# Four small transfers of a triangular inverse, issued from GpSimd's queue in place of SyncE's, in a one-core decoder layer

## The chip, the cores and the metric

The kernel runs on one core of one Trainium2 chip. The metric is the time of one execution on the device in microseconds; lower is better. The kernel before ran three times: 2893.89, 2886.44 and 2890.0 us, median 2890.0 us.

## What is computed

One layer of a hybrid decoder, for a prompt of 512 tokens and a sample group of 8 sequences with 4 tokens each (544 columns together), all in float32 with D = 2048. Cut to the part that the change touches, the gated DeltaNet heads:

```python
decay = jnp.exp(jnp.where(incl, cum[..., :, None] - cum[..., None, :], -jnp.inf))
kk = jnp.einsum('nbhid,nbhjd->nbhij', kc, kc)
lower = jnp.where(strict, bc[..., :, None] * kk * decay, 0.0)
rhs = jnp.concatenate([vc * bc[..., None], kc * (bc * jnp.exp(cum))[..., None]], axis=-1)
sol = lax.linalg.triangular_solve(lower + jnp.eye(c, dtype=f32), rhs, left_side=True, lower=True, unit_diagonal=True)
...
def step(state, inp):
    u_i, w_i, qk_i, q_i, k_i, g_i = inp
    v_new = u_i - jnp.einsum('bhcd,bhde->bhce', w_i, state)
    o_i = jnp.einsum('bhcd,bhde->bhce', q_i, state) + jnp.einsum('bhij,bhje->bhie', qk_i, v_new)
    state = g_i * state + jnp.einsum('bhcd,bhce->bhde', k_i, v_new)
    return state, o_i
```

Around it stand one combined projection, stick-breaking attention with 8 heads, the output projection, a cross attention over 256 memory tokens and a SwiGLU block.

## The kernel before

Activations lie transposed, 128 features on the partitions and 544 tokens along the free dimension. A product with a float32 weight is made of three float32r products (high times high, high times low, low times high). `weights` loads 512 KB of a weight at a time from SyncE's queue (L201), ScalarE casts the high part (`wh`, L206), VectorE subtracts it for the low part (`wl`, L207), and `products` issues the matmuls (L218). There are three raw buffers and four of each part, so that the load of a piece waits for VectorE to be done with an older one.

The dense projections set the pace. Everything else of a head is a generator (`sb_head`, `gdn_head`, `gdn_sample`, `sb_sample`) that the class `Side` steps forward between matmuls: each `yield cost, lat` names the TensorE time that the step took and a latency in microseconds before which its next step isn't taken. With it the program text puts the side work among the projections; the instructions then stand in one fixed order on each engine, and an engine that comes to an instruction whose input is missing waits there, with everything behind it.

`gdn_head` runs for 8 heads (called head 0 to head 7 here), between about 490 and 1000 us of the span. For each it makes the 128 x 128 matrices of four chunks (`gt`, L1087 and L1088) and calls `invert`, which calls `invert16` for the 16 x 16 blocks on the diagonal. `invert16` needs the 32 blocks (4 chunks with 8 blocks each) with one block on each partition. It gets them by way of DRAM:

- L890: GpSimd copies identities into `t`, half of the tile `g16`.
- L892: `gt` (128 partitions, 4 x 128 values each) is written to the scratch array `scr[0]`, 256 KB.
- L894: the 32 diagonal blocks are read back to `g`, 32 partitions with 16 rows of 16 values, 32 KB.
- L896: GpSimd changes the sign.
- L899 and L900: VectorE solves the blocks row by row, 15 multiplications and 15 reductions, interleaved with its other work.
- L903: the solved blocks are written to the diagonal of `scr[1]` or `scr[2]` (zero elsewhere), 32 KB.
- L906: the whole array is read back to the tile `T`, 256 KB, followed by `yield 0.0, 8`.
- L924: TensorE transposes `T`; ScalarE copies it to `TT` (L926), and the levels 16, 32 and 64 are built from it by matmuls (L960 and L965).

Each of L894, L903 and L906 waits for what stands before it: the transfer before, or VectorE. All four go out on SyncE's queue, which also issues the weights (L201), the cache pages (L787) and the states of the sample group. GpSimd's queue holds in this stretch the product of the gate `cv` (L870, the end of a SiLU), small clears (L1020, the three columns ahead of a convolution, read by L1035), copies of the convolution's tail (L1026), `qd` (L1074), the decay products (L1087, L1092), clears of the windows for the sample values (L740) and the convolution of the sample group (L1168, L1170). The only transfers on GpSimd's queue are those of L2126 in the SwiGLU stage, after 2383 us.

Of the kernel before, what the change touches and what calls it, by code (L numbers as in the profile page):

```python
# [51 lines left out]
def bc(ap, shape):  # L52
    return ap.broadcast_to(shape)
# [819 lines left out]
def invert16(c, gt):  # L873

    nc = c.nc
    gt16 = c.tt("g16")
    g, t, prod = gt16[:32, 0:256], gt16[:32, 256:512], c.tt("p16")[:32]
    src, dst = c.scr[0], c.scr[1 + c.inv % 2]  # L880
    c.inv += 1

    def whole(x):
        return x.rearrange("(a x) -> a x", a=4)[:, : P * P].rearrange("a (j i) -> j a i", i=P)

    def blocks(x):
        return x.rearrange("(n x) -> n x", n=32)[:, : 16 * P].rearrange("n (r i) -> n r i", i=P)[:, :, :16]

    gv, tv = (x.rearrange("p (r i) -> p r i", r=16) for x in (g, t))
    nc.gpsimd.tensor_copy(t, c.id16)  # L890
    yield 0.0, 1.0
    nc.sync.dma_start(whole(src), v3(gt))  # L892
    yield 0.0, 2.5
    nc.sync.dma_start(gv, blocks(src))  # L894
    yield 0.0, 2.5
    nc.gpsimd.tensor_scalar(g, g, -1.0, None, ALU.mult)  # L896
    for i in range(1, 16):
        p3 = prod[:, : i * i].rearrange("p (n j) -> p n j", n=i)
        nc.vector.tensor_mul(p3, tv[:, :i, :i].rearrange("p j n -> p n j"), bc(gv[:, :i, i : i + 1].rearrange("p j o -> p o j"), [32, i, i]))  # L899
        nc.vector.tensor_reduce(tv[:, i, :i], p3, mybir.AxisListType.X, ALU.add)  # L900
        if i % 4 == 3:
            yield 0.0, 1.2 + i / 8
    nc.sync.dma_start(blocks(dst), tv)  # L903
    yield 0.0, 2.5
    tr = c.tt("T")
    nc.sync.dma_start(v3(tr), whole(dst))  # L906
    yield 0.0, 8
    return tr


def invert(c, gt, nc_, levels, res):
# [17 lines left out]
    if levels[0] == 16:  # L929
        tr = yield from invert16(c, gt)  # L930
        tt = transposed(tr)
    else:
        ps = transposes(c, gt, nc_)
        tr, tt = c.tt("T"), c.tt("TT")
        nc.vector.tensor_mul(v3(tr, nc_), v3(ps, nc_), wide(c.m1))
        nc.vector.tensor_sub(v3(tr, nc_), wide(c.ident), v3(tr, nc_))
        nc.gpsimd.tensor_mul(v3(tt, nc_), gv, wide(c.m1t))
        nc.gpsimd.tensor_sub(v3(tt, nc_), wide(c.ident), v3(tt, nc_))
# [54 lines left out]
def v3(t, n=4):  # L993
    return t[:, : n * P].rearrange("p (a d) -> p a d", a=n)
# [1441 lines left out]
```

## Time and profile before

| what | value |
|---|---|
| three runs | 2893.89, 2886.44, 2890.0 us; median 2890.0 |
| profiled execution, its own time | 2890.46 us |
| its span, first to last instruction | 2888.8 us |
| mean granted clock of TensorE | 0.996 of full speed |
| TensorE matmul busy | 2825.7 us, 98% of the span |
| weight load busy (beside the matmuls) | 2717.5 us, 94% |
| VectorE busy | 2013.4 us, 70% |
| ScalarE busy | 1447.1 us, 50% |
| GpSimd busy | 728.0 us, 25% |
| hardware queue of SyncE (q1) | 600600 packets, 384.64 MB |
| software queue (q0) | 22176 packets, 42.90 MB |

The table is read from the top: the span is nearly filled by TensorE, and the rest of the engines stand beside it. A wait counts where it ends a wait of TensorE. Times in the sections below count from the start of the span; the letter q behind an engine's name (SPq, POOLq) marks its instruction queue, and PEld is TensorE's weight load, which goes ahead of each matmul.

### The profile page before, as it was taken

To read this page: it belongs to the slowest core of one execution; us is meant where nothing else is said; L and a number is where in the kernel's file an instruction comes from. 1 tells how busy PE (TensorE), PEld (TensorE's weight loads), DVE (VectorE), ACT (ScalarE), POOL (GpSimd) and SP (SyncE) were. 2 spreads that over 40 slices of the span, in tenths; PEclk is the share of its full clock that TensorE was granted. 3 is DMA by queue.
4 is the path that set the end of the run, shared out by engine and by line. 5 is a ranking of instruction groups with operands and counts; after the bars stand their busy time and mean duration, and the time that the engine had idled before them with its cause. 6 is when DMAs were issued, how large, how long until landed. Compare 5 with 4: busy or idle time off the path is not lost. (4 is left out here: it accounts for less than half of the span.)

```text
span 2888.8 us, 57077 instructions
## 1 busy us (share of the span) xinstructions
PE 2825.7 (98%) x22442; PEld 2717.5 (94%) x22442; DVE 2013.4 (70%) x3168; ACT 1447.1 (50%) x2760; POOL 728.0 (25%) x858
## 2 busy tenths in 40 slices
PE   8999999999999999999989999999999999999998
PEld 7998888888989999999789999999999999999998
DVE  5554435577777654446588888888888887888886
ACT  5445435454444354434654444444444446555675
POOL 3122212123213110003333333433433334121200
PEclk9999999999999999999999999999999999999999
DMA  7334453544342464533535455545545559876653
GB/s 227 98 90 136 132 155 116 157 118 141 109 135 87 138 202 149 152 101 104 189 121 161 146 154 174 168 148 165 164 146 157 157 152 274 246 223 182 198 166 91
DMA packets 632693, 442.72 MB, mean 153 GB/s; under 512 B 36107, under 2 KB 559704, under 8 KB 632424
## 3 DMA queue, kind: packets, MB, share of 16 engines
q1 hardware_dynamic: 600600, 384.64, 44.8%
q0 software_dynamic: 22176, 42.90, 4.8%
q10 hardware_dynamic: 9648, 11.54, 1.1%
q8 instruction: 176, 2.88, 0.4%
q14 instruction: 93, 0.76, 0.1%
HBM read 359.23 MB, written 79.75 MB: 152 GB/s over the span
## 5 line engine op out<-in xcount | busy, mean ns | idle before, releaser
L2061 PE MATMUL gu<-pr,wh 128*128 128x272 f32 x4944 | 675.1, 289 | 6.7 <-ACT pr L1690 3.0
L2061 PEld LDWEIGHTS gu<-pr,wh 128*128 128x128 f32 x4944 | 643.4, 189 | 8.4 <-ACT pr L1690 3.4
L218 PE MATMUL mm<-ah,wh 128*128 128x272 f32 (+1 forms) x2464 | 542.2, 300 | 6.5 <-ACT ah L334 4.2
L218 PE MATMUL mm<-al,wh 128*128 128x272 f32 (+1 forms) x2464 | 519.6, 290 | 0.7 <-DVE al L249 0.7
L218 PE MATMUL mm<-ah,wl 128*128 128x272 f32 (+1 forms) x2464 | 513.8, 289 | 0.1
L1941 PE MATMUL bank<-pr,wh 128*128 128x272 f32 x2464 | 466.5, 289 | 0.9 <-ACT bank L1969 0.9
L207 DVE TENSOR_TENSOR wl<-wr,wh 128x512 fp32r<-128x512 f32 (+1 forms) x340 | 244.1, 721 | 239.8 <-ACT wh L206 228.6
L218 PEld LDWEIGHTS mm<-ah,wh 128*128 128x128 f32 (+1 forms) x2464 | 386.6, 188 | 25.8 <-issue 12.1
L218 PEld LDWEIGHTS mm<-al,wh 128*128 128x128 f32 (+1 forms) x2464 | 388.1, 188 | 3.0 <-DVE al L249 0.9
L1941 PEld LDWEIGHTS bank<-pr,wh 128*128 128x128 f32 x2464 | 386.3, 188 | 2.9 <-ACT bank L1969 2.7
L218 PEld LDWEIGHTS mm<-ah,wl 128*128 128x128 f32 (+1 forms) x2464 | 385.2, 188 | 3.2 <-issue 1.7
L2061 PE MATMUL gu<-pr,wl 128*128 128x272 f32 x2472 | 362.9, 289 | 1.9 <-issue 1.8
L206 ACT CAST wh<-wr 128x512 fp32r<-128x512 f32 (+1 forms) x340 | 207.7, 614 | 307.9 <-PE mm L218 255.4
L1941 PE MATMUL bank<-pr,wl 128*128 128x272 f32 x1232 | 354.8, 288 | 0.0
L2061 PEld LDWEIGHTS gu<-pr,wl 128*128 128x128 f32 x2472 | 330.6, 189 | 2.3 <-issue 2.0
L1839 DVE TENSOR_TENSOR wl<-sum,wh 128x1024 fp32r<-128x1024 f32 x172 | 220.3, 1281 | 76.9 <-ACT wh L1835 76.9
L1941 PEld LDWEIGHTS bank<-pr,wl 128*128 128x128 f32 x1232 | 232.0, 188 | 0.0
L1835 ACT CAST wh<-sum 128x1024 fp32r<-128x1024 f32 x172 | 180.4, 1049 | 78.3 <-PE gu L2061 47.2
L1839 DVE TENSOR_TENSOR wl<-raw,wh 128x1024 fp32r<-128x1024 f32 x133 | 202.2, 1521 | 15.4 <-ACT wh L1835 13.5
L1835 ACT CAST wh<-raw 128x1024 fp32r<-128x1024 f32 x133 | 139.9, 1052 | 102.4 <-PE gu L2061 93.1
L2126 POOL DMA_DIRECT2D pr<-hT x154 | 81.8, 546 | 254.1 <-PE bank L1941 229.2
L1828 DVE TENSOR_TENSOR sum<-raw,sum 128x1024 f32<-128x1024 f32 x86 | 135.8, 1579 | 0.9
(530 smaller groups left out, 4152.5 us busy)
## 6 DMA issues: line engine op xcount, KB each, us to landing
raw<-in_w_gate_up SPq DMA_DIRECT2D x176, 512.0 KB
wr<-in_w_in SPq DMA_DIRECT2D x108, 512.0 KB
raw<-in_w_down SPq DMA_DIRECT2D x176, 256.0 KB
hT<-hs SPq DMA_DIRECT2D x154, 272.0 KB
pr<-hT POOLq DMA_DIRECT2D x154, 272.0 KB, 6.5
page<-in_cache_sb_k SPq DMA_DIRECT2D x128, 128.0 KB
page<-in_cache_sb_v SPq DMA_DIRECT2D x64, 256.0 KB
wr<-in_w_out SPq DMA_DIRECT2D x32, 512.0 KB
```

The costliest lines, as they stand in the source:

```text
L206: nc.scalar.copy(hi[:, :m, :n], raw[:, k : k + m, :n])
L207: nc.vector.tensor_sub(lo[:, :m, :n], raw[:, k : k + m, :n], hi[:, :m, :n].bitcast(F32))
L218: c.nc.tensor.matmul(ps[:n, h, :HT], l[:, :n], r[:, h * HT : (h + 1) * HT], start=first and i == 0, stop=last and i == 2,)
L1828: self.f.c.nc.vector.tensor_sub(self.a[q], self.a[x], self.a[y])
L1835: self.f.c.nc.scalar.copy(self.hi[q], self.left(q))
L1839: self.f.c.nc.vector.tensor_sub(self.lo[q], self.left(q), self.hi[q].bitcast(F32))
L1941: self.c.nc.tensor.matmul(self.c.bank[bank][:, o], t[x][:, s, i * P : (i + 1) * P], pairs[i].op[q][r], start=new and not (i or n), stop=se ...
L2061: self.c.nc.tensor.matmul(bank, w[:, i * P : (i + 1) * P], self.pairs[i].op[q][r], start=start and n == 0, stop=n == 23, skip_group_check= ...
L2126: self.c.nc.gpsimd.dma_start(t, self.hT[2 * g + pair, :, max(0, 2 * n - 1) + k])
```

## The change

The four calls in `invert16` are issued by `nc.gpsimd` in place of `nc.sync`. Shapes, scratch arrays, waits and the steps of the generator stay as they are.

```diff
     nc.gpsimd.tensor_copy(t, c.id16)
     yield 0.0, 1.0
-    nc.sync.dma_start(whole(src), v3(gt))
+    nc.gpsimd.dma_start(whole(src), v3(gt))
     yield 0.0, 2.5
-    nc.sync.dma_start(gv, blocks(src))
+    nc.gpsimd.dma_start(gv, blocks(src))
     yield 0.0, 2.5
     nc.gpsimd.tensor_scalar(g, g, -1.0, None, ALU.mult)
 ...
-    nc.sync.dma_start(blocks(dst), tv)
+    nc.gpsimd.dma_start(blocks(dst), tv)
     yield 0.0, 2.5
     tr = c.tt("T")
-    nc.sync.dma_start(v3(tr), whole(dst))
+    nc.gpsimd.dma_start(v3(tr), whole(dst))
     yield 0.0, 8
     return tr
```

The 32 transfers leave SyncE's queue and stand in GpSimd's. On SyncE, at the end of head 5's inversion, the piece of the difference is (`scr` is the scratch array, `wr` a raw weight, `cumrow` the decay row of the next head, `out<-st` a state that is stored):

```order
 L1135 DMA out<-st 128x128
-L201 DMA wr<-in_w_in 128x8x128 x2
-L903 DMA scr_4207<-g_10321 32x16x16
-L201 DMA wr<-in_w_in 128x8x128
-L906 DMA T<-scr_4207 128x4x128
+L201 DMA wr<-in_w_in 128x8x128 x3
 L1054 DMA cumrow<-cum_rows 128x512
```

The weight load and the row that stood between and behind the two transfers follow one another now.

On GpSimd, at the end of head 1's inversion (first) the two transfers come to stand ahead of the clears of two windows, `win`:

```order
 L1020 MEMSET cr 128x3
 L1026 COPY convp<-cr 128x3
+L903 DMA scr_4207<-g_7310 32x16x16
+L906 DMA T<-scr_4207 128x4x128
 L740 MEMSET win 128x16x16 x2
 L870 TENSOR_TENSOR cv<-cv,l 128x512
```

The windows' clears, and the product behind them, are reached now only when L906 has been issued. The same end of head 5's inversion on GpSimd reads:

```order
 L1026 COPY convp<-cr 128x3
 L870 TENSOR_TENSOR cv<-cv,l 128x512
+L903 DMA scr_4207<-g_10321 32x16x16
+L906 DMA T<-scr_4207 128x4x128
 L1020 MEMSET cr 128x3
 L1026 COPY convp<-cr 128x3
```

Here it is the clear of the next convolution's first columns that stands behind both.

The order of TensorE's own work is nearly the same: of the eight places where `T` is transposed, only head 5's is another:

```order
 L218 MATMUL mm<-ah,wh 128x272 x2
-L218 MATMUL mm<-al,wh 128x272
+L218 MATMUL mm<-al,wh 128x272 x2
+L218 MATMUL mm<-ah,wl 128x272
 L924 MATMUL aux<-ident,T 128x128 x4
 L979 MATMUL aux<-ident,cv 128x128 x8
 L960 MATMUL aux<-T,gt 128x128 x4
```

Two of the projection's matmuls have moved from behind the transposes to ahead of them.

## Rows read from the trace of the kernel before

**Rows 1.** Busy time in the stretch from 500 to 980 us, which holds the inversions of all eight heads: length, then busy us of TensorE's matmuls and weight loads, VectorE, ScalarE and GpSimd (with the count of instructions), the granted clock, the busy share of the DMA engines, GB/s.

```profile
500.00:980.00 480.00, 466.02 (x3844) 433.54 (x3844) 332.22 (x853) 227.82 (x606) 116.99 (x162) 1.00 0.43 126
```

**Rows 2.** Who waited for whom between 500 and 980 us: us in total, times, the longest. The first two are the only waits of a computing engine for a DMA in that answer, beside a second row for the matmuls of the same L924.

```profile
POOL g L896 <- DMA g<-scr: 23.1, 7, 6.4
PEld aux L924 <- DMA T<-scr: 2.7, 1, 2.7
ACT wh L206 <- PE mm L218: 88.0, 54, 5.8
```

**Rows 3.** SyncE's queue in order of time: the issues of L903 in heads 0 to 7, with L906 of heads 5 and 7. Columns: start, length of the issue.

```profile
532.40 0.34 SPq L903 DMA_DIRECT2D scr<-g  x1
...
604.19 0.33 SPq L903 DMA_DIRECT2D scr<-g  x1
...
658.23 0.33 SPq L903 DMA_DIRECT2D scr<-g  x1
...
719.47 0.33 SPq L903 DMA_DIRECT2D scr<-g  x1
...
776.70 1.05 SPq L903 DMA_DIRECT2D scr<-g  x1
...
853.71 0.33 SPq L903 DMA_DIRECT2D scr<-g  x1
...
855.52 0.37 SPq L906 DMA_DIRECT2D T<-scr  x1
...
905.27 0.33 SPq L903 DMA_DIRECT2D scr<-g  x1
...
963.10 0.33 SPq L903 DMA_DIRECT2D scr<-g  x1
...
964.84 0.57 SPq L906 DMA_DIRECT2D T<-scr  x1
```

**Rows 4.** TensorE's weight loads in order of time: the transposes of `T` (L924) in heads 0 to 7. Columns: start, length; in brackets the idle time before and what ended it.

```profile
548.15 0.47 PEld L924 LDWEIGHTS aux<-ident,T 128*128 128x128 f32 x4
...
614.16 0.48 PEld L924 LDWEIGHTS aux<-ident,T 128*128 128x128 f32 x4
...
672.78 0.48 PEld L924 LDWEIGHTS aux<-ident,T 128*128 128x128 f32 x4
...
734.40 0.47 PEld L924 LDWEIGHTS aux<-ident,T 128*128 128x128 f32 x4
...
786.64 0.51 PEld L924 LDWEIGHTS aux<-ident,T 128*128 128x128 f32 x4
...
859.83 0.71 PEld L924 LDWEIGHTS aux<-ident,T 128*128 128x128 f32 x4 [2.67 <-DMA T<-scr]
...
916.38 0.47 PEld L924 LDWEIGHTS aux<-ident,T 128*128 128x128 f32 x4
...
972.41 0.47 PEld L924 LDWEIGHTS aux<-ident,T 128*128 128x128 f32 x4
```

**Rows 5.** TensorE around that wait: the stretch behind it (length, busy us, granted clock, DMA share, GB/s), and the four transposes of head 5 and of head 6.

```profile
859.80:863.20 3.40, 3.37 (x16) 0.51 0.02 5
...
859.84 1.11 PE L924 MATMUL aux<-ident,T 128*128 128x128 f32 x4 [2.45 <-DMA T<-scr]
...
916.49 0.60 PE L924 MATMUL aux<-ident,T 128*128 128x128 f32 x4
```

**Rows 6.** The transfers of GpSimd's queue in the SwiGLU stage, L2126 (272 KB each, 128 partitions with one piece of 2176 bytes): ns of an issue (least, median, greatest), first and last start; then us from issue to landing.

```profile
L2126 POOL DMA_DIRECT2D pr<-hT x154: 527/535/764, 2383.6 to 2751.4; - x154
...
DMA to landing us min/median/max: 2.9/6.5/8.8
```

**Rows 7.** The front part of head 4's inversion in order of time: two issues on SyncE's queue, two instructions of GpSimd, and VectorE's first of L899.

```profile
749.57 1.37 POOL L1092 TENSOR_TENSOR cumrow<-cumrow,sm 128x512 f32<-128x512 f32 x1
...
756.33 0.84 POOL L896 TENSOR_SCALAR g<-g 32x256 f32<-32x256 f32 x1
...
750.92 0.37 SPq L892 DMA_DIRECT2D scr<-gt  x1
753.27 0.33 SPq L894 DMA_DIRECT2D g<-scr  x1
...
761.18 0.15 DVE L899 TENSOR_TENSOR p<-g 32x1 f32<-32x1 f32 x1
```

**Rows 8.** What stands behind L903 and L906 on GpSimd after the change, and who needs it, in order of time: head 1 (the clears of the windows, ScalarE's last two copies into them, TensorE's use), then head 5 (the clear, the convolution's first step, the gate's product, and TensorE's transposes of it).

```profile
601.46 0.56 POOL L740 MEMSET win<- 128x256 f32 x2
...
609.57 0.48 ACT L743 COPY win<-z 128x128 f32<-128x128 f32 x2
...
611.66 1.06 PE L762 MATMUL aux<-page,win 128*32 128x512 f32 x8
...
849.61 0.10 POOL L1020 MEMSET cr<- 128x3 f32 x1
...
856.21 0.72 ACT L1035 ACTIVATE cv<-cr,convw 128x512 f32<-128x512 f32 x1 [0.46 <-DVE wl L207]
...
864.60 1.30 POOL L870 TENSOR_TENSOR cv<-cv,l 128x512 f32<-128x512 f32 x1 [9.46 <-ACT l L869]
...
870.73 0.60 PE L979 MATMUL aux<-ident,cv 128*128 128x128 f32 x4
```

**Rows 9.** What SyncE's queue waited for between 500 and 1000 us, the row of L903.

```profile
SPq L903 <- DVE g L900: 29.1, 7, 9.3
```

## The prediction

> **What bounds the kernel now.** I read the page first. The table by engine says that matmuls fill 98% of the span, so only a change in what TensorE waits for can move the time. Next I took the stretch that holds the eight inversions, by busy time: TensorE is busy for 466.0 of 480 us [rows 1], so whatever is mended there can give back at most 14.0 us, 0.5% of the kernel. Then the list of waits in that stretch, to see whether TensorE waits for the transfers that move. It does once, 2.7 us for `T` [rows 2]. GpSimd waits for `g` seven times, 23.1 us in all, but nobody waits for GpSimd's L896 behind it. No engine that computes waits for a weight or a cache page: ScalarE's cast waits for TensorE to free a buffer, 88.0 us in 54 waits [rows 2]. So the weights are early throughout, and SyncE is not what holds the kernel.
>
> The last view is the order of time, for the distance of each head from its write of solved blocks (L903) to the transposes of `T` (L924). From L903's issue to the weight load of L924 it is 15.75, 9.97, 14.55, 14.93, 9.94, 6.12, 11.11 and 9.31 us in heads 0 to 7 [rows 3, 4]. In head 5 2.67 us of the 6.12 are the wait, so TensorE was ready 3.45 us after L903 and the two transfers took 6.12: 1.81 from L903 to L906, 4.31 from L906 to the transposes [rows 3, 4]. That is the one inversion whose transfers set TensorE's pace. The wait costs more than itself: from 859.8 to 863.2 us the granted clock is 0.51, the 1.2 GHz level, behind a stretch in which TensorE had little to do, and four transposes take 1.11 us in place of 0.60 [rows 5]. Of 3.40 us at 0.51 about 1.7 are lost. Head 5's late `T` costs 2.7 + 1.7 = 4.4 us now.
>
> **The change part by part.** Nothing is computed differently; 32 issues leave SyncE and 32 come to GpSimd.
>
> *SyncE's queue, freed.* It loses 32 issues of some 0.35 us and the waits at them, of which that of L903 for VectorE is the dearest: 29.1 us in seven waits [rows 9]. The weights and pages behind them go out earlier. I cost this at nothing, because what hides it is the early weights above: nobody waits for either. If that cover were gone it could not give more than the 14.0 us.
>
> *The price of an issue on GpSimd.* The kernel's own transfers there occupy GpSimd for a median of 535 ns [rows 6], against 0.33 and 0.37 us on SyncE [rows 3]. They have 128 pieces; the four here have 512 each (128 partitions with 4 rows, or 32 with 16). The lower bound is the same 0.53 us, that is 0.20 and 0.16 us more than on SyncE for L903 and L906. The upper bound is a price by the piece, 4 x 0.535 = 2.14 us, that is 1.8 more for each. No row lies between them; I take 0.9 more, the half of the upper surcharge. The Trainium skill, DMA: Bandwidth & Descriptors (section Latency and other measured facts), gives about 0.6 us to the first byte for the queues of SyncE and ScalarE and about 1 us for GpSimd's; by that estimate the surcharge would be 0.4 for each transfer, and head 5's wait would grow by 0.6 us. The surcharge from rows is taken.
>
> *The back half, L903 to `T`.* The shortest pair on SyncE is 1.74 us from L903 to L906, in head 7, and the one landing of `T` that shows is 4.31 us [rows 3, 4]. With 0.9 us on each the chain is 1.74 + 0.9 + 4.31 + 0.9 = 7.85 us. At that time GpSimd has nothing to do in head 5: its last instruction is over at 849.7, and L903 goes at 853.7 [rows 3, 8]. Against the distances above, 7.85 fits into every head but the sixth. There TensorE's ready time of 3.45 us grows by 0.25, since two more matmuls now stand ahead of the transposes (466.0 us for 3844 matmuls is 0.12 each [rows 1]). The wait becomes 7.85 - 3.70 = 4.15 us in place of 2.67, **+1.5 us**. The clock falls as before; no new cost. With the lower surcharge the chain is 6.41 and head 5 waits 2.71, no change; with the upper one it is 9.63, head 5 waits 5.93 (+3.3) and head 7 waits 0.3: +3.6 in all.
>
> *The front half, L892 to L896.* Head 4 has the least room: `g` is changed in sign from 756.33 to 757.17, and VectorE's first L899 comes at 761.18, 4.0 us later [rows 7]. GpSimd is done with L1092 at 750.94 and SyncE issued L892 at 750.92, so the new queue begins no later. Two surcharges of 0.9 take 1.8 of the 4.0 us, the upper ones 3.6. Price nothing, hidden by VectorE's other work up to L899; were it gone, the solve and with it L903 would slip by as much.
>
> *What is held behind the waits on GpSimd.* L906 waits on GpSimd for L903's landing, and the work behind it with it. Head 1: the windows' clears, at 601.46 before, cannot start until 604.19 + 2.64 + 1.27 = 608.1 and end at 608.7; ScalarE's last copies into the windows ended at 610.05 and TensorE wants them at 611.66 [rows 3, 8], so 0.7 us of delay find 1.6 of room. With the upper surcharge the clears end at 604.19 + 3.55 + 2.14 + 0.56 = 610.4 and the room is about used up. Head 5: the clear for the next convolution moves from 849.61 to 853.71 + 2.64 + 1.27 = 857.6, ScalarE's L1035 from 856.21 to 857.7, 1.5 us late; the product at its end was over at 865.9, and TensorE wants it at 870.73 [rows 8], 4.8 us later. Price nothing in both.
>
> *Sum.* +1.5 us on the profiled execution: 2890.46 + 1.5 = **2892.0 us**. That execution lies 0.5 above the median of the three runs, so it stands for them.
>
> **The rivals.**
>
> *`T` comes earlier.* On SyncE the transfer of `T` stood behind a weight of 512 KB; on GpSimd it has a queue of its own. If it lands as the quickest of that queue do, 2.9 us [rows 6], the chain is 1.74 + 0.2 + 2.9 = 4.84, and head 5 still waits 1.1; if the chain falls to 3.7, the wait and the clock's fall go away: 2890.5 - 4.4 = 2886.1. For it speaks that the DMA engines are 43% busy on the mean [rows 1]; against it that the weight now goes out at the same moment, and that the median landing of that queue is 6.5.
>
> *Slower: the transfers take long enough to reach other heads.* Let an issue cost the upper 2.14 us and `T` land as the median of rows 6 does, with 1.6 more for its pieces: 1.74 + 1.81 + 6.5 + 1.6 = 11.65 us. Then head 5 waits 7.95 (5.3 more), and heads 1, 4, 6 and 7 wait 1.7, 1.7, 0.5 and 2.3, 11.5 together; with one more fall of the clock, 1.7, the time is about 2904. It shows as more than 0.3% (8.7 us) from a chain of 11 us on. For it: nothing in the trace shows 512 pieces from GpSimd. Against: those landings were taken with eight transfers of 272 KB on the way together. A form of it is that VectorE, busy for 332 of 480 us here [rows 1], keeps GpSimd from writing its descriptors. The rows speak against a large price: with VectorE at work beside it the longest issue of the 154 is 0.764 us, 0.23 above the median [rows 6]; twice that gives a chain of 8.3 and 2892.5. The Trainium skill, SBUF — State Buffer (section SBUF: two separate sides), states the rule: while VectorE runs an instruction in a two-port mode, GpSimd can't write the descriptors of its transfers, and the queues of SyncE and ScalarE are free of this. Its section A bandwidth-pool intuition that's wrong (but worth ruling out) has about 620 ns alone and 3100 beside such an instruction; that estimate, 2.5 us on each, would put 5 us on the chain and the time at 2908 to 2913.
>
> *Faster: SyncE's freedom counts after all.* If weights or pages were late somewhere that the waits hide, at most the 14.0 us of TensorE that is not busy come back: 2876.5. Against it stand all of rows 2.
>
> **How the numbers follow.** A measurement of this kernel can tell about 0.3%, 8.7 us, from no change. The forecast has 0.65, the earlier `T` 0.13, the slower rival 0.18, the freed SyncE 0.04. The first two lie within 0.3%: same 0.78, slower 0.18, faster 0.04. The range takes the earlier `T` (2886.1) less a little for the scatter of the runs, 2885, and reaches at the top to the slower rival, 2904; beyond it are left the worse half of that rival and the freed SyncE, 0.13.
>
> **What would show it.** Right: head 5's transposes wait 3 to 5 us for `T`, the other seven at most some tenths; the issues on GpSimd last between 0.5 and 2.1 us; L896 comes 1 to 3 us later and nobody waits for it; the casts still wait for TensorE and not for a weight. Wrong: an issue on GpSimd far over 2 us, a landing of `T` over 6 us, waits for `T` in heads 1, 4 and 7, or VectorE waiting for `g`. The sum is wrong, too, if TensorE's lost time is found outside of the stretch of the inversions.

## The result and the profile after

The changed kernel takes 2893.91 us (median of 20 runs, 2890.45 to 2902.79); the kernel before, run beside it, 2890.64 (20 runs, 2886.16 to 2895.59). The ratio is 1.0016, 95% interval 1.0010 to 1.0022, that is 4.6 us more (2.9 to 6.4; the two medians lie 3.3 apart): a small loss, within the 0.3% of "no change". The forecast was 2892.0 with a range of 2885 to 2904, so the class and the range held and the sum, +1.5 us, fell short.

The profiled execution takes 2890.45 us, which is the quickest of the 20, against 2890.46 before. So the spans say nothing about the change: it has to be read inside the stretch of the inversions. Two markers around that stretch do it, a matmul ahead of the first inversion (L556) and one behind head 5's (L1109). First the kernel before, then the changed one (start, duration, instruction):

```profile
485.35 0.40 PE L556 MATMUL aux<-sp,sfxr 128*128 128x512 f32 x1
...
899.12 0.49 PE L1109 MATMUL aux<-st,cv 128*128 128x128 f32 x2 [0.71 <-DVE st L1126]
```

```profile
486.03 0.40 PE L556 MATMUL aux<-sp,sfxr 128*128 128x512 f32 x1
...
902.46 0.49 PE L1109 MATMUL aux<-st,cv 128*128 128x128 f32 x2
```

TensorE is 0.68 us behind at the first and 3.34 at the second: between them the change cost 2.7 us in this execution. Behind 1000 us the changed kernel's execution gets it back where nothing was changed, in good part because the granted clock happened to fall less there (1.00 and 0.97 from 1350 to 1400 and from 1450 to 1500 us, against 0.97 and 0.93 before).

The waits of the changed kernel from 500 to 980 us (who waits, for whom, us in all, times, longest) answer to [rows 2]:

```profile
ACT wh L206 <- PE mm L218: 77.2, 53, 6.0
...
POOL g L896 <- DMA g<-scr: 15.4, 7, 3.6
...
POOL g L894 <- DMA scr<-gt: 14.5, 8, 2.6
...
POOL T L906 <- DMA scr<-g: 9.0, 4, 4.0
...
ACT cv L1035 <- POOL cr L1020: 6.4, 3, 4.1
...
PEld aux L924 <- DMA T<-scr: 4.7, 1, 4.7
```

Three things are to be seen. The one wait for `T` has grown from 2.7 to 4.7 us, still in head 5 alone. GpSimd itself now waits for transfers in L894 and L906. And ScalarE waits for a clear on GpSimd (L1020), a wait that the kernel before doesn't have: somebody does wait behind GpSimd.

Head 5, the changed kernel on GpSimd, TensorE's weight load and SyncE's queue (start, duration, [idle before <- releaser]):

```profile
856.60 0.71 POOL L903 DMA_DIRECT2D scr<-g  x1 [4.52 <-DVE g L900]
861.30 0.78 POOL L906 DMA_DIRECT2D T<-scr  x1 [3.99 <-DMA scr<-g]
862.08 0.12 POOL L1020 MEMSET cr<- 128x3 f32 x1
```

```profile
864.52 0.72 PEld L924 LDWEIGHTS aux<-ident,T 128*128 128x128 f32 x4 [4.69 <-DMA T<-scr]
```

```profile
856.64 0.37 SPq L201 DMA_DIRECT2D wr<-in_w_in  x1
857.19 0.44 SPq L1054 DMA_DIRECT2D cumrow<-cum_rows  x1
```

From L903 to the transposes it is 7.92 us, in place of 6.12 [rows 3, 4]. But the parts are not those of the forecast: 4.70 us to L906 and 3.22 from there, where SyncE took 1.81 and 4.31. The 32 KB write has become slow and `T` quick. And SyncE, no longer held by L903, sends a weight of 512 KB 0.04 us behind the start of an issue that lasts 0.71 us.

One of the signs that the prediction named for being wrong did show, at a place where it costs nothing: a landing of `T` over 6 us. The eight took 3.2 to 6.8 us (median 3.7); the slowest is head 2's, with four cache pages (L787) sent within 1.3 us of it, and TensorE comes to its transposes only 11 us behind L906.

Head 0, first GpSimd, then ScalarE, then TensorE in the changed kernel:

```profile
512.11 0.99 POOL L892 DMA_DIRECT2D scr<-gt  x1
515.70 0.68 POOL L894 DMA_DIRECT2D g<-scr  x1 [2.59 <-DMA scr<-gt]
518.55 0.85 POOL L896 TENSOR_SCALAR g<-g 32x256 f32<-32x256 f32 x1 [2.17 <-DMA g<-scr]
519.36 0.09 POOL L1020 MEMSET cr<- 128x3 f32 x1
```

```profile
519.49 0.72 ACT L1035 ACTIVATE cv<-cr,convw 128x512 f32<-128x512 f32 x1 [2.06 <-POOL cr L1020]
...
523.14 0.57 ACT L709 COPY kT<-aux 128x512 f32<-128x512 f32 x1
```

```profile
523.76 0.43 PE L720 MATMUL aux<-kT,win 128*32 128x128 f32 x8 [0.58 <-ACT kT L709]
...
539.38 0.43 PE L720 MATMUL aux<-kT,win 128*32 128x128 f32 x8 [0.35 <-ACT kT L709]
```

and the first two in the kernel before:

```profile
516.18 0.09 POOL L1020 MEMSET cr<- 128x3 f32 x1
```

```profile
517.10 0.72 ACT L1035 ACTIVATE cv<-cr,convw 128x512 f32<-128x512 f32 x1 [0.33 <-DVE raws L1023]
...
520.93 0.57 ACT L709 COPY kT<-aux 128x512 f32<-128x512 f32 x1
```

The clear stands behind L896, L896 behind two transfers. It comes 3.2 us later; the convolution's L1035 2.4 us later; the copy of the keys `kT`, which needs nothing of this but stands behind it on ScalarE, 2.2 us later (0.7 of each is the lag that was there before); and TensorE waits for `kT` twice, 0.58 and 0.35 us, 0.9 together.

### The profile page after: what moved, and what is told of

The parts are those of the page before. It is cut to its first block, busy times and chain, and to the rows that moved or that the text cites. A ratio compares the mean times of both kernels' runs of the same rounds, so it can differ in the third digit from the quotient of the medians.

```text
span 2888.6 us, 57093 instructions
## 1 busy us (share of the span) xinstructions
PE 2823.9 (98%) x22442; PEld 2715.2 (94%) x22442; DVE 2012.9 (70%) x3168; ACT 1446.4 (50%) x2760; POOL 750.7 (26%) x890
## 5 line engine op out<-in xcount | busy, mean ns | idle before, releaser
L2126 POOL DMA_DIRECT2D pr<-hT x154 | 81.8, 549 | 254.2 <-PE bank L1941 192.8
```

Source lines behind the costliest of these rows:

```text
L2126: self.c.nc.gpsimd.dma_start(t, self.hT[2 * g + pair, :, max(0, 2 * n - 1) + k])
```

## Experiments

Theory T1: the loss comes from two places, the weight that delays head 5's write, and GpSimd's waits that hold the clear L1020. Rival R1: GpSimd's queue is itself slow with these transfers, wherever they stand. Rival R2: only the clock of other stages differs.

### The two halves apart

Back half only, and front half only, each with the other two lines as in the kernel before:

```diff
# back half
-    nc.sync.dma_start(blocks(dst), tv)
+    nc.gpsimd.dma_start(blocks(dst), tv)
-    nc.sync.dma_start(v3(tr), whole(dst))
+    nc.gpsimd.dma_start(v3(tr), whole(dst))
# front half
-    nc.sync.dma_start(whole(src), v3(gt))
+    nc.gpsimd.dma_start(whole(src), v3(gt))
-    nc.sync.dma_start(gv, blocks(src))
+    nc.gpsimd.dma_start(gv, blocks(src))
```

Back half. 

> Only the back half moves: L903 and L906 on GpSimd, L892 and L894 on SyncE. Theory T1: the change's 4.6 us come from two places. In head 5 the 512 KB weight (L201) goes out from the freed SyncE in the 0.7 us in which GpSimd still writes L903's descriptors, the 32 KB write falls behind it and lands 4.2 us after its issue in place of about 2.3; in head 0 the waits of GpSimd for the front half hold the clear L1020, and behind it ScalarE's L1035 and L709, and TensorE's L720. By T1 head 5 stays as in the changed kernel (4.7 us from L903 to L906, a wait for T of about 4.6), head 0's waits of L720 for kT are gone, and the time is 2.5 to 3.5 us over before. Rival R1: GpSimd's queue is itself slow with these 512 pieces, and that alone makes the 4.6 us: then head 5 is the same and the time 4 to 5 us over before. Rival R2: the two kernels differ only by the clock that other stages were granted: then the time is within 1 us of before.

Front half. 

> Only the front half moves: L892 and L894 on GpSimd, L903 and L906 on SyncE. T1: head 5 is back at 1.8 us from L903 to L906 and a wait for T of about 2.7; in head 0 ScalarE's L1035 waits about 2 us for the clear L1020 and TensorE's L720 about 0.9 us for kT in two places; the time is 1 to 2 us over before. R1: the front half has room everywhere, so the time is within 0.5 us of before, and no wait for kT shows. R2: within 1 us of before.

Measured: 1.0003 (0.9994 to 1.0012) and 1.0009 (0.9998 to 1.0019) of before. Neither time is told from no change, so they don't judge; the traces do. The back half alone has head 5's long chain (write 4.80 us, wait for `T` 5.05) and nothing in head 0; the front half alone has head 0's waits (0.97 us of `L720` for `kT` at 521.64) and in head 5 a write of 1.77 us, a wait of 3.41 (2.7 was expected; `T`, on SyncE, took 5.12 us there). The stretch from 500 to 560 us, which holds head 0 (length, then busy us of TensorE's matmuls and weight loads, VectorE, ScalarE, GpSimd, clock, DMA share, GB/s), in the back half alone and in the front half alone:

```profile
500.00:560.00 60.00, 60.00 (x568) 52.65 (x568) 33.85 (x75) 31.15 (x72) 10.06 (x16) 1.00 0.53 154
```

```profile
500.00:560.00 60.00, 58.70 (x560) 51.61 (x559) 33.50 (x74) 29.44 (x66) 10.34 (x15) 1.00 0.53 151
```

The front half takes 1.3 us of TensorE there, the back half none. The changed kernel has 59.06 in that row and the kernel before 60.00. So time is lost in the inversions themselves, and R2 falls in its strict form, that only the clock differs. That a part of the 4.6 us is clock isn't excluded: the time of the back half alone, 0.9 us over before, is what R2 forecast, and 2.5 to 3.5 was what T1 did.

The front half has a further, smaller price. Between 540 and 850 us TensorE falls back by another 0.7 to 0.8 us, in steps at about 652 and 753 us, in the changed kernel, with the front half alone and in the run of the next section, and not with the back half alone. It isn't traced further here.

### Head 0's front half back on SyncE

```diff
-    nc.gpsimd.dma_start(whole(src), v3(gt))
+    (nc.sync if c.inv == 1 else nc.gpsimd).dma_start(whole(src), v3(gt))
-    nc.gpsimd.dma_start(gv, blocks(src))
+    (nc.sync if c.inv == 1 else nc.gpsimd).dma_start(gv, blocks(src))
```

> The changed kernel with L892 and L894 back on SyncE in head 0 alone; TensorE's order of instructions is the changed kernel's. T1 (the held clear L1020 makes ScalarE's L1035 and the key copies L709 late in head 0): no wait of L720 for kT at about 522 and 538 us, TensorE stands at 850 us 1.5 to 2.2 us earlier than in the changed kernel, head 5 as there (4.7 us from L903 to L906, wait about 4.7); the time is 2 to 3 us over before. R1 (the front half costs nothing, all is the queue's price in head 5): TensorE stands at 850 us where the changed kernel has it within 0.3 us, and the time is 4 to 5 us over before.

Measured: TensorE is busy for 60.00 of the 60 us again and no wait for `kT` is left, so the hold of head 0 is shown, at 0.9 us. Head 5 is as in the changed kernel (4.43 us to L906, wait 4.49). The time, 1.0018 (1.0009 to 1.0027), 5.2 us over before (2.6 to 7.8), doesn't show the gain: 0.9 us is less than these intervals can tell. At 850 us TensorE stands 1.1 us earlier than in the changed kernel, less than T1 expected (1.5 to 2.2) and more than R1 (0.3).

### What makes head 5's write slow

Three kernels, all with the four transfers on GpSimd. The first two put 64-byte transfers on SyncE at the old places, to hold it as before (only the added transfers are shown):

```diff
# row held: two holds
+    nc.sync.dma_start(hold[0:1, :16], tv[0:1, 15, :])            # behind L903
+    nc.sync.dma_start(hold[1:2, :16], blocks(dst)[0:1, 15, :])   # behind L906
# second kernel: one hold
+    nc.sync.dma_start(hold[0:1, :16], blocks(dst)[0:1, 15, :])   # behind L903
```

> All four on GpSimd as in the changed kernel, and SyncE is held at the two old places by a 64-byte transfer each: one waits for VectorE's solve, as L903 did, one for the landing of the write, as L906 did. In head 5 the weight still goes out within 0.6 us of L903, but the 256 KB decay row (L1054) only when the write has landed. T1 in the form that the weight is what delays the write: 4.3 us or more from L903 to L906, wait for T 4 to 5 us. T1 in the form that the row delays it: under 3 us from L903 to L906, wait for T 2.5 to 3.5. R1: 4.7 us and 4.7 us, as in the changed kernel.

> All four on GpSimd, and one 64-byte transfer on SyncE at L903's old place that reads what L903 wrote, so that the weight and the decay row behind it go out only when the write has landed. T1 (either form): 2.4 to 2.9 us from L903 to L906 in head 5, as in heads 1 to 3 of the changed kernel; T then travels beside the weight and takes 3.2 to 4.3 us to the transposes, and the wait for T is 2.5 to 3.9 us. R1: 4.7 us from L903 to L906, wait for T about 4.7.

Measured: 4.73 us to L906 and a wait of 6.29 with the decay row held, so the row isn't the cause (the wait is longer than in the changed kernel, since `T` now travels beside the row: 4.79 us from L906). The second kernel was a miss: 4.57 us, a wait of 6.14, but the weight went out at 856.64, ahead of the hold at 860.64, since the program had put the waiting transfer behind it on SyncE. It doesn't test what it was made for. So the weight was bound to the write by its own buffer (the condition is put in words; the kernel counts the weights issued from L903 on):

```diff
 raw = c.w.tile([P, 8, P], F32, tag="wr", name="wr", bufs=3)
+if this_is_the_weight_beside_head_5s_write:
+    nc.sync.dma_start(raw[0:1, 0, :16], blocks(dst)[0:1, 15, :])
 nc.sync.dma_start(raw, w[...])
```

> The changed kernel, and ahead of the one weight that goes out beside head 5's write a 64-byte transfer from what L903 wrote into the weight's own buffer: so this weight (512 KB) and the decay row behind it start only when the write has landed. T1 (the weight, issued within 0.05 us of L903, delays the write): in head 5 2.4 to 2.9 us from L903 to L906, as in heads 1 to 3 of the changed kernel, and a wait for T of 2.0 to 3.2 us. R1 (GpSimd's queue itself is slow there): 4.7 us from L903 to L906 and a wait of 4.7.

Its rows of GpSimd, TensorE's weight load and SyncE:

```profile
859.09 0.71 POOL L903 DMA_DIRECT2D scr<-g  x1 [4.53 <-DVE g L900]
861.76 0.79 POOL L906 DMA_DIRECT2D T<-scr  x1 [1.97 <-DMA scr<-g]
```

```profile
865.15 0.42 PEld L924 LDWEIGHTS aux<-ident,T 128*128 128x128 f32 x4 [2.84 <-DMA T<-scr]
```

```profile
862.75 0.37 SPq L201 DMA_DIRECT2D wr<-in_w_in  x1
```

With the weight behind it the write takes 2.67 us, and the wait for `T` is 2.84, nearly that of the kernel before [rows 4]. GpSimd still issues all four. In the seven runs that send this weight within 0.1 us of the start of L903 on GpSimd, the write takes 4.43 to 4.80 us. This run holds the decay row too, but the row held alone left 4.73. R1 falls in head 5; the weight is the cause. (One run of it has a time, 2896.22 us, which says little.)

### `T` alone on GpSimd

```diff
-    nc.sync.dma_start(v3(tr), whole(dst))
+    nc.gpsimd.dma_start(v3(tr), whole(dst))
```

> Only L906, the reading of T, goes to GpSimd; L892, L894 and L903 stay on SyncE. T1: the write is ahead of the weight in SyncE's own queue and lands as in the kernel before (1.8 to 2.4 us from L903 to L906, the weight beside it notwithstanding), and T on a queue of its own takes 3.2 to 3.5 us from L906 to the transposes in place of 4.3; head 5 waits 1.5 to 2.3 us for T, nothing is lost in head 0, and the time is between 1.5 us less than before and the same. R1: GpSimd's queue makes head 5 late whichever transfer it carries: 4 us or more of wait, 1 to 3 us over before.

Measured: 0.9991 (0.9983 to 1.0000). The write, ahead of the weight in SyncE's own queue, takes 2.25 us to L906 though the weight follows 0.57 us behind it. But `T` takes 4.66 us to the transposes and not 3.2 to 3.5, and the wait is 3.31, between what T1 and R1 expected. Here the weight was sent 1.7 us ahead of `T` and the decay row 1.2 ahead; in the changed kernel they were 4.7 and 4.1 ahead (3.22 us), with the weight held 1.0 and 1.5 behind (3.39), and on SyncE before the weight was 1.3 ahead (4.31). So `T`'s time goes by what else is under way, more than by the queue. The move of this one transfer costs nothing that the runs can tell, which speaks against R1.

### More room ahead of head 5's transposes

The step ahead of the transposes is given more time, in head 5 only, on SyncE and in the changed kernel:

```diff
-    yield 0.0, 8
+    yield 0.0, 12 if dst is c.scr[2] and c.inv == 6 else 8     # or 20
     return tr
```

12 us on SyncE. 

> The kernel before (all four on SyncE), and head 5's step ahead of the transposes of T is given 12 us in place of 8, so that they come later in TensorE's order. T1 (head 5's late T costs 2.7 us of wait and 1.7 of clock in the kernel before): no wait for T anywhere, no fall of the clock at 860 us, 3 to 4.5 us less than before. Rival: the work that is now ahead of the transposes is taken from behind them, and a later wait of the same chain grows by as much: within 1.5 us of before.

12 us in the changed kernel. 

> The changed kernel with the same 12 us in head 5. T1: no wait for T though the write still lands 4 us after L903; what is left over the sibling on SyncE is head 0's hold, 1 to 2 us, so 2 to 3.5 us less than before. R1 (each transfer on GpSimd costs, wherever it stands): still 2 us or more above the sibling without a wait that shows why. Rival: a later wait takes the place, within 1.5 us of the changed kernel.

12 us on SyncE with `T` alone on GpSimd. 

> The version with 12 us in head 5 (four transfers on SyncE, 3.9 us less than before) with L906 alone moved to GpSimd. T1: T arrives 0.8 to 1.5 us earlier, head 5 waits 1 to 2 us in place of 2.7, no fall of the clock, and the time is 4 to 6 us less than before. R1: the move costs as it did in the changed kernel: 0 to 2 us less than before.

20 us on SyncE. 

> The kernel before, with 20 us in place of 8 ahead of head 5's transposes of T. With 12 us the wait for T was still 2.7 us, since no matmul came between the ready time and T, and only the fall of the clock behind it was gone (3.9 us less). T1: 20 us put some 8 us of matmuls more ahead of the transposes, the wait for T is gone in every head and the clock keeps its level, 5 to 7 us less than before. Rival: the chain behind T (three more levels, the decay of the next chunk) is now what TensorE waits for: waits of 2 us or more in L924 for TT or L1109 for st, and 1 to 4 us less than before.

20 us in the changed kernel. 

> The changed kernel with 20 us in place of 8 ahead of head 5's transposes of T. T1 (the change costs time only where TensorE waits for T in head 5 and in head 0): the write of head 5 still lands about 4 us after L903, but nobody waits for T; head 0's L720 still waits for kT in two places; the time is 2 to 4 us less than before, 1 to 2 us over its sibling on SyncE (0.998 of before). R1 (GpSimd's queue costs wherever it stands): within 1 us of before or above it.

| kernel | of before | wait for `T` in head 5 | clock 860 to 865 us |
|---|---|---|---|
| 12, SyncE | 0.9986 (0.9977 to 0.9995) | 2.69 | 1.00 |
| 12, changed | 1.0013 (1.0004 to 1.0022) | 4.71 | 0.63 |
| 12, `T` alone | 0.9991 (0.9981 to 1.0000) | 3.00 | 0.66 |
| 20, SyncE | 0.9980 (0.9971 to 0.9989) | none | 1.00 |
| 20, changed | 1.0012 (1.0001 to 1.0022) | none | 1.00 |

With 12 us the transposes traded places with other work, but the wait stayed: T1's "no wait" failed in the first two, and its 1 to 2 us in the third. On SyncE the clock kept its full level in spite of a wait as long as before, and some 4 us are gained (1.4 to 6.6). With `T` alone on GpSimd the wait was 3.00 us and the clock fell again, behind the same order of TensorE's work; the times of these two can't be told apart. TensorE's transposes with 12 us on SyncE, then with `T` alone:

```profile
858.10 0.65 PE L924 MATMUL aux<-ident,T 128*128 128x128 f32 x4 [2.47 <-DMA T<-scr]
```

```profile
860.94 1.12 PE L924 MATMUL aux<-ident,T 128*128 128x128 f32 x4 [2.79 <-DMA T<-scr]
```

The changed kernel with 12 us lies 0.27%, 7.8 us, above its sibling on SyncE, where T1 expected 1 to 2. The traces account for 6.3 of it: 2.0 of wait for `T`, 3.4 of clock (0.66 against 1.00 from 860 to 870 us) and 0.9 of head 0.

With 20 us the wait for `T` is gone on both queues, and this was the test that T1 lost: on SyncE 5.8 us are gained (3.2 to 8.4), in the changed kernel 3.5 lost. So the change costs some 9 us here (0.32%; the ends of the two intervals leave 0.12 to 0.51%), though head 5's transposes wait for no transfer. By the time alone R1 was right: it expected no less than before, T1 2 to 4 us less. The trace of the changed kernel with 20 us shows where: GpSimd, ScalarE, TensorE.

```profile
856.45 0.71 POOL L903 DMA_DIRECT2D scr<-g  x1 [4.53 <-DVE g L900]
861.17 0.78 POOL L906 DMA_DIRECT2D T<-scr  x1 [4.01 <-PE mm L218]
861.94 0.12 POOL L1020 MEMSET cr<- 128x3 f32 x1
861.99 0.20 POOL L1026 COPY convp<-cr 128x3 f32<-128x3 f32 x1
869.12 1.26 POOL L870 TENSOR_TENSOR cv<-cv,l 128x512 f32<-128x512 f32 x1 [6.93 <-ACT l L869]
```

```profile
862.10 0.72 ACT L1035 ACTIVATE cv<-cr,convw 128x512 f32<-128x512 f32 x1 [3.81 <-POOL cr L1020]
```

```profile
870.44 1.11 PE L979 MATMUL aux<-ident,cv 128*128 128x128 f32 x4 [4.03 <-POOL cv L870]
```

On SyncE the same places read:

```profile
848.03 0.10 POOL L1020 MEMSET cr<- 128x3 f32 x1
...
861.28 1.29 POOL L870 TENSOR_TENSOR cv<-cv,l 128x512 f32<-128x512 f32 x1 [7.73 <-ACT l L869]
```

```profile
862.63 0.66 PE L979 MATMUL aux<-ident,cv 128*128 128x128 f32 x4 [0.16 <-POOL cv L870]
```

The clear L1020 of the next head's convolution, a tenth of a microsecond of work, stands behind L906, which waits for the slow write. The product L870 comes 7.8 us later than on SyncE, 3.8 of it a lag that TensorE already has at 752 us (head 0's hold is part of that), and TensorE waits 4.0 us for `cv`. The releaser named at L906 is a matmul; it goes 4.7 us behind L903 as in the other kernels with the weight beside the write, so the landing is the likelier one. So T1 had the right two causes and places too few: the hold of head 0 exists in head 5 as well, and in the changed kernel the wait for `T` covers it.

The slow write shows in a second head, too. With 20 us in the changed kernel head 7's transposes wait 1.45 us for `T`, on SyncE 0.17:

```profile
989.31 0.42 PEld L924 LDWEIGHTS aux<-ident,T 128*128 128x128 f32 x4 [1.45 <-DMA T<-scr]
```

```profile
981.06 0.42 PEld L924 LDWEIGHTS aux<-ident,T 128*128 128x128 f32 x4 [0.17 <-DMA T<-scr]
```

There a weight went out 1.3 us ahead of the write, and L906 came 5.94 us behind L903; on SyncE, with a weight 1.2 ahead, 5.13. So a write behind a weight is slow on either queue.

In these two executions the lag grows from 1.9 us at 485 us, ahead of the first moved transfer, to 3.8 at 752 (1.3 of the growth is head 0's hold), 7.8 at 870, 9.0 behind the clock's fall at the new wait (0.84 from 870 to 880 us), 7.0 at 906 and, with head 7's wait, 8.3 at 989. The change made 6.4 us of it.

The kernel with 20 us on SyncE beats both of the case.

## Why the prediction was right, and where its sum was not

*The view and the place were right.* The only wait for a moved transfer that sets TensorE's pace is head 5's, the other seven inversions have room, and the stretch bounds the effect. The class, within 0.3%, came from there.

*The price of an issue.* The bounds, 0.53 and 2.14 us, held: the 32 issues take 0.67 to 0.99 us. The surcharge over SyncE is 0.38 us for L903 (0.71 against 0.33) and 0.42 for L906 (0.79 against 0.37); 0.9 was taken. The estimate from the Trainium skill, DMA: Bandwidth & Descriptors, 0.4 for each, comes nearer, though what the page gives is the time to the first byte and not the length of an issue; the 0.6 us that it gave for head 5 is too small, because the issue is not what grew most. The rule of the Trainium skill, SBUF — State Buffer (section SBUF: two separate sides), that VectorE in a two-port mode stops GpSimd's descriptors, shows in none of the 32: none is over 0.99 us, beside a VectorE that is busy for 331 of 480 us. Why is not tested here.

*The chain of the back half* was forecast at 7.85 us and is 7.92, by luck: 1.74 + 0.9 for the write was 2.06 us too little (4.70), and 4.31 + 0.9 for `T` 1.99 too much (3.22). TensorE was ready 3.23 us after L903 and not 3.70, so the wait is 4.69 in place of 4.15. The term of +1.5 us is +2.0.

*SyncE freed, at nothing.* That nobody gains from early weights was right. The step looked for a gain alone; what was missed is what the freed queue sends, and when: the weight now starts inside the 0.7 us for which GpSimd's issue lasts, and the small write on the critical chain pays 2 us. The weight's hold shows this. The Trainium skill, DMA: Bandwidth & Descriptors (section Issuing engines are not separate DMA queues), says that all issuing engines end on the same 16 DMA engines and interleave there; the trace agrees, 4.70 us beside the weight and 2.67 without it. The rival "`T` earlier" rested on a queue of its own, against that rule: the part that came true, 3.22 us, was the weight being through.

*Held behind the waits on GpSimd, at nothing.* **This is the step that failed.** It looked at the back half only, in heads 1 and 5, and there at the direct reader. In head 0 the front half's two transfers hold L1020, and the loss reaches TensorE over ScalarE's queue, through a copy that has no part in the convolution: 0.9 us. In head 5 ScalarE's L1035 was forecast 1.5 us late and is 6.0 (862.23 against 856.21, 2.4 of it a lag that TensorE has by then). The price was nothing, as forecast, but the cover was the wait for `T` itself; without it the same hold costs 4 us of waiting, as the run with 20 us shows.

*The front half, hidden* was right for VectorE, which never waits for `g`.

*The clock.* "No new cost" holds in the profiled execution: head 5's fall costs about what it did (0.83 from 860 to 870 us, 0.84 before). What stays open is the rest of the size: in the profiled execution the inversions lost 2.7 us, by the runs it is 4.6 (2.9 to 6.4). A candidate was seen and not settled. Behind the later wait of `L924` for `TT` (1.6 to 1.9 us in all of these kernels) the clock falls in some executions and not in others: from 880 to 895 us it is 1.00 before, in the changed kernel and with the front half alone, but 0.77 with the back half alone, where TensorE has 91 matmuls recorded in place of 121:

```profile
880.00:895.00 15.00, 13.73 (x91) 13.05 (x92) 9.17 (x23) 5.91 (x12) 3.01 (x6) 0.77 0.21 56
```

With that fall the back half alone lost 4.5 us between the two markers of the result, more than the whole change did without it. What decides it, and how often it happens in the runs without a profile, no run tells.

## What to carry to other kernels

A transfer that is moved to a compute engine's queue brings its wait with it. List everything behind that wait, down to clears of a tenth of a microsecond, and follow each over the queues of its readers until an engine that sets the pace is reached; room that is only another wait is no room.
Ask of the queue that is freed what it will send at that moment: a large early load that comes out beside a small transfer on the critical chain costs more than the dearer issue.

## What the runs showed of the hardware

- An issue on GpSimd lasted 0.81 us for the 256 KB out of 128 partitions, 0.67 for the 32 KB in, 0.71 for the 32 KB out and 0.79 for the 256 KB in (512 pieces each); the 128 pieces of [rows 6] took 0.53. The price did not go by the piece.
- The 32 KB write landed 2.3 us after its issue on GpSimd in the median of the eight heads and 4.2 beside a weight that went out 0.04 us behind the issue's start. In heads 0 to 2, where a weight followed 0.8 to 1.1 us behind, it took 2.67 to 2.68 us to L906, as with the weight held back (2.67). The weight isn't the only load that counts: in head 4, where a load of states (L1266) went out 0.08 us ahead and a weight 1.2 behind, L906 came 3.88 us behind L903.
- A wait of 2.7 us ahead of four transposes was followed by a fall of the clock to 0.68 from 860 to 865 us in the kernel before and by none in the one with 12 us (1.00), where matmuls of 272 columns stand behind the transposes and not further transposes. That order alone isn't the reason: with `T` alone on GpSimd and 12 us the same matmuls stand there, and behind a wait of 3.0 us the clock fell (0.66). What decides, no run tells.
